# An encoder block of two SwiGLUs and a mixer on one core: two block products of four units ahead at the head of each SwiGLU, norms written in place on VectorE with four tiles in flight, and the shared accumulator of the down-projection added in pieces

## The chip, the cores and the metric

The kernel runs on one core of a Trainium2 chip. The metric is the device time of one execution in microseconds (us); a smaller one is better. A core has a matrix engine (TensorE, PE in the profile; its weight loads are PEld), VectorE (DVE), ScalarE (ACT), GpSimd (POOL) and SyncE (SP), which issues the transfers between HBM and the on-chip memory SBUF. Products of PE land in banks of a second on-chip memory, PSUM, and another engine reads ("evacuates") them from there. Each engine works through its own queue in order and waits on semaphores for the others.

## The reference

One layer over x of 1024 tokens by 1024 columns, fp32 in and out, with a hidden width of 2816:

```python
h = x
f1 = swiglu(rms_norm(h, ffn1_pre_g), ffn1_w_gate, ffn1_w_up, ffn1_w_down)
h = h + 0.5 * rms_norm(f1, ffn1_post_g)
mix = hybrid_mixer(rms_norm(h, mix_pre_g), ...)   # two kinds of attention, gated, projected
h = h + rms_norm(mix, mix_post_g)
f2 = swiglu(rms_norm(h, ffn2_pre_g), ffn2_w_gate, ffn2_w_up, ffn2_w_down)
h = h + 0.5 * rms_norm(f2, ffn2_post_g)

def rms_norm(x, g): return x * rsqrt(mean(x * x) + EPS) * g
def swiglu(x, w_gate, w_up, w_down): return (silu(x @ w_gate) * (x @ w_up)) @ w_down
```

## The kernel before, in words

The 1024 tokens are eight tiles of 128. Each fp32 matrix is split into a high and a low part of a shorter format (`xh` and `xl`, two halves of `wt`), and a product is three matmuls per pair of operands: high by high, high by low, low by high.

**Gate and up.** The 2816 columns of the gate and of the up matrix are 11 column pairs of 256; a pair of one of the two matrices is a unit (p, m), so a SwiGLU (FFN1, FFN2) has 22. A unit is computed with seven block products instead of eight (a Strassen-Winograd scheme over 2x2 blocks of x and of the weight). A product, numbered 0 to 6, is 12 matmuls of 128x512. Products 0 and 1 need only the upper half of x, that is token tiles 0 to 3, and weight blocks as loaded; the others need the lower half (block 2) or sums and differences of blocks (4, 5, 6, 3, made by `XS.put`, L414, and of the weight, L615 to L626). A weight block is cast to its high part by ACT (L648), and its low part is a subtraction on DVE (L649). Sums of the seven results are made on DVE (L697, L760 to L800), and the hidden values are written to HBM and read back for the down-projection. At the head of a SwiGLU the order is product 0 of units 0 and 1, product 1 of units 0 and 1, and then unit by unit.

**Making x.** A pre-norm takes a tile: ACT squares it with a sum (L441), POOL makes `rstd` from the sum (L307, L309), and the tile is scaled by `rstd` and the gain: DVE does the first columns (`on_dve`, L451) and ACT with POOL the rest (`on_pool`, L457, L458). PE transposes the scaled tile in blocks of 128x128 into a PSUM bank (L426), ACT copies out the high part (`xh`, L430), DVE subtracts for the low part (`xl`, L431), and the bank is free. There are four single banks (`B1`) and two double ones.

**Down.** Five groups of seven block products (order 0, 5, 1, 4, 6, 2, 3), each for four pairs of token tiles, are added into eight accumulators `acc` (1024 columns a tile) and a shared `bacc` of 512 columns, which belongs into three quarters of a tile pair's output. After the last group `fix` adds it: DVE to one half of tile tt (L1037), POOL to both halves of tile tt + 4 (L1039). What is left of the depth follows as 16 plain products of six matmuls (L283), one for each tile and column half, which DVE adds into `acc` (L1118).

**Turns.** When a tile of a SwiGLU or of the mixer is done, `postnorm` squares it (ACT, L499), multiplies it by its gain into a new tile `xn` (L488, some columns on POOL and the others on DVE), and adds it, scaled by `rstd`, to the residue `res` (DVE, L512, a scalar_tensor_tensor, STT). A pre-norm of the new residue for the next part follows. `norm_tok` lets two tiles be between these steps at a time.

**What sets the order.** The program is written as generators, one for each chain of steps. A planner, `Plan`, plays them through with costs for each engine's steps and ranks, and the order in which it starts them is the order of the program. Buffers are taken in that order from pools: 4 KB slots (`slot`), half slots, big slots for `xh` and `xl`. A changed cost, rank or number of tokens so moves instructions in every queue.

Of the kernel before, what the change touches and what calls it, by code (L numbers as in the profile page):

```python
# [10 lines left out]
F32R = mybir.dt.float32r  # L11
# [96 lines left out]
PRE1, PREM, PRE2 = 768, 768, D  # L108
POOL1, POOLM, POOL2 = [512] * 8, [384] * 8, [512] * 4 + [1024, 768, 512, 512]
# [3 lines left out]
HELD = 4  # L113

# [105 lines left out]
def _build(tc, es, a, consts, out, dbg):  # L220
# [133 lines left out]
    class XS:  # L354
# [25 lines left out]
        def put(self, t, xn, scaled, rank):  # L380
# [15 lines left out]
            else:  # L396
# [14 lines left out]
                tt = [slot([P, 2, 512], name="xt") for _ in range(2)]  # L411
                t1, t2, t3, t4 = tt[0][:, 0, :], tt[0][:, 1, :], tt[1][:, 0, :], tt[1][:, 1, :]
# [21 lines left out]
    def prenorm(src, g, X, t, rank, split_at, xn=None):  # L434
# [12 lines left out]
        m = split_at  # L447
        scaled = [Event(), Event((m > 512) + (m < D))]

        def on_dve(c0, c1, ev):  # L450
# [5 lines left out]
        def on_pool(c0, c1, ev):  # L456
            yield act(c1 - c0, lambda: A.mul(xn[:, c0:c1], src[:, c0:c1], rs[0]))  # L457
            yield pool(c1 - c0, lambda: G.tensor_mul(xn[:, c0:c1], xn[:, c0:c1], g()[:, c0:c1]))  # L458
            plan.set(ev)
# [11 lines left out]
    def postnorm(y, g, res_src, dst, t, box, junk, pool_cols, parts=1):  # L471
# [10 lines left out]

        m = pool_cols(t)
        gained = Event((m > 0) + (m < D))

        def gain_of(cols, eng):
            def write():
                eng.tensor_mul(xn[:, cols], y[:, cols], g()[:, cols])  # L488

            n = cols.stop - cols.start  # L490
            yield (pool if eng is G else dve)(n, write)
            plan.set(gained)

        xn = slot([P, D], name="xn")
        box.append(xn)
# [6 lines left out]
        if m:  # L502
            spawn(gain_of(slice(0, m), G), 0)
        if m < D:
            spawn(gain_of(slice(m, D), V), 8)
        yield act(D + 100, sq)
        yield from rstd_steps(bx[0], D, rs)
        yield gained
        n = D // parts
        for q in range(parts):  # L510
            cs = slice(n * q, n * q + n)
            yield dve(n, lambda: V.scalar_tensor_tensor(res[:, cs], xn[:, cs], rs[0], res[:, cs], op0=ALU.mult, op1=ALU.add))  # L512
            spawn(store(dst[t * P : (t + 1) * P, cs], res[:, cs], 512 // parts), 6)
# [30 lines left out]
    def ffn(X, wg, wu, wd, post, hs, hp, started=None, room=None):  # L544
        raw_tok, w_tok, hl_tok = Tokens(4 if room is None else 3), Tokens(6 if room is None else 2), Tokens(3)

        def more():
            yield room
            plan.release(raw_tok, 1)
            plan.release(w_tok, 4)  # L550
# [7 lines left out]
        seq = [(units[0], 0), (units[1], 0), (units[0], 1), (units[1], 1)]  # L558
        for n, u in enumerate(units):
            if n > 1:  # L560
# [3 lines left out]
            if n > 1:  # L564
# [5 lines left out]
        unit_tok = Tokens(2)  # L570
# [13 lines left out]
        def loads():  # L584
            yield 0.5
            for p, m in units:
# [11 lines left out]
        def prep():  # L598
            sums = {}

            def begin(u):
# [5 lines left out]
                bx.used = used = [Event(4), Event(4)]  # L607
# [29 lines left out]

            def one(u, i):
# [17 lines left out]
            for u, i in seq:  # L656
                if u not in sums:
                    begin(u)
                if i == 1:
# [55 lines left out]
        def step(u, i, ub):  # L715
# [21 lines left out]
            if i == 0:  # L737
# [16 lines left out]
            elif i == 5:  # L754
# [3 lines left out]
                def first():  # L758
                    yield ub.m1
                    yield dve(512, lambda: V.tensor_add(u2(), ub.b6, u2()))  # L760
# [128 lines left out]
        fixed = [Event() for _ in range(NT)]  # L889
# [133 lines left out]
        def evac(g, i, tt, ps, ev, tok):  # L1023
# [8 lines left out]
            if g == NGR - 1 and i == 3:  # L1032
                spawn(fix(tt), 2)
# [11 lines left out]
        pdone = [Event() for _ in range(4)]  # L1045

        def down():
            for g in range(NGR):
                evs = {}
                banks = {}  # L1050
                for s, i in enumerate(ORDER):
# [4 lines left out]
                    for tt in range(4):  # L1056
# [27 lines left out]
                        if g == NGR - 1 and i == 2:  # L1084
                            e = evs[i, tt] = pdone[tt]
# [85 lines left out]
    def begin():  # L1171
        def one(t):
# [9 lines left out]
            yield from prenorm(bx[0], lambda: gb["g1"], X1, t, 3, PRE1)  # L1182
# [12 lines left out]
    norm_tok = Tokens(2)  # L1195

    def post1(y, t):
# [8 lines left out]
        yield from postnorm(y, lambda: gb["p1"], a["x"], h1, t, bx, lambda: gb["j1"], POOL1.__getitem__)  # L1206
        yield from prenorm(bx[0], lambda: gb["gm"], Xm, t, 3, PREM, bx[1])
# [1193 lines left out]
    def merge():  # L2401
# [109 lines left out]
        def tail(y, t, ev):  # L2511
# [3 lines left out]
            yield from postnorm(y, lambda: gb["pm"], h1, h2, t, bx, lambda: gb["jm"], POOLM.__getitem__)  # L2515
            yield from prenorm(bx[0], lambda: gb["g2"], X2, t, 3, PRE2, bx[1])
# [97 lines left out]
```

## Time and profile before

| | |
|---|---|
| median of 3 runs | 2476.06 us (2475.08 to 2478.7) |
| the profiled execution | 2472.7 us, of which its span 2470.5 us |
| PE busy | 2310.1 us (94%) |
| DVE busy | 1602.3 us (65%) |
| ACT busy | 1042.7 us (42%) |
| POOL busy | 798.0 us (32%) |

The span is the time from the first to the last instruction in the trace; all positions in this document are microseconds from its start. FFN1's gate and up stand at 0 to 470, its down-projection at 470 to 707, the mixer (with attention) up to 1772, FFN2's gate and up from 1726 to 2206, its down-projection and the last norms to the end.

### The profile page before, as it was taken

The page shows a single profiled execution, that of the slowest core. Times are in us where ns is not written, and L with a number is a line of the kernel's source. Part 1 is how long each engine was busy: PE and PEld are TensorE (multiplying, and loading weights), DVE is VectorE, ACT ScalarE, POOL GpSimd, SP SyncE. Part 2 cuts the span into 40 slices and gives each one's busy share as a digit, 9 for nine tenths or more (in the row PEclk, how much of TensorE's full clock was granted, in tenths as well). Part 3 has the DMA queues.
Part 4 walks back from the last instruction along what each step waited for, and adds up shares of the span by engine and source line. Part 5 has one row for each costly group of instructions (what it writes and reads, how often), then busy time and mean ns, then how long its engine had stood idle before and what let it go on. Part 6 is the DMA issues. An engine that isn't in the chain of part 4 may idle for free. (4 is left out here: it accounts for less than half of the span.)

```text
span 2470.5 us, 30753 instructions
## 1 busy us (share of the span) xinstructions
PE 2310.1 (94%) x11096; PEld 1928.9 (78%) x11096; DVE 1602.3 (65%) x2667; ACT 1042.7 (42%) x1966; POOL 798.0 (32%) x600
## 2 busy tenths in 40 slices
PE   6999999999979999999998898988889999998996
PEld 4888888778869987888887777766678888877885
DVE  7887877756582105665666767258877877774657
ACT  6343434332153336666664555455343433433211
POOL 2000000354384445665623223566200000023535
PEclk8999999999989999999999999999989999999998
DMA  4243443677342132131232323665333534447762
GB/s 154 103 168 131 170 154 128 244 307 267 135 164 76 60 103 92 38 83 50 66 97 67 85 74 98 206 242 193 131 124 128 183 128 153 162 179 289 286 216 102
DMA packets 188823, 360.64 MB, mean 146 GB/s; under 512 B 32448, under 2 KB 104640, under 8 KB 188160
## 3 DMA queue, kind: packets, MB, share of 16 engines
q1 hardware_dynamic: 188672, 358.69, 42.5%
q8 instruction: 87, 1.43, 0.2%
q14 instruction: 64, 0.52, 0.1%
HBM read 237.92 MB, written 120.72 MB: 145 GB/s over the span
## 5 line engine op out<-in xcount | busy, mean ns | idle before, releaser
L675 PE MATMUL s<-xh,wt 128*128 128x512 f32 x1408 | 452.3, 392 | 13.2 <-DVE uu L771 12.2
L522 POOL TENSOR_TENSOR wdb<-rawd,wdb 128x1024 fp32r<-128x1024 f32 x34 | 87.0, 2562 | 957.9 <-ACT wdb L521 957.9
L675 PE MATMUL b<-xh,wt 128*128 128x512 f32 x1056 | 344.1, 393 | 1.8 <-DVE wt L649 0.8
L675 PEld LDWEIGHTS s<-xh,wt 128*128 128x128 f32 x1408 | 265.9, 189 | 71.9 <-issue 13.3
L675 PE MATMUL s<-xl,wt 128*128 128x512 f32 x704 | 275.4, 391 | 0.0
L675 PEld LDWEIGHTS b<-xh,wt 128*128 128x128 f32 x1056 | 199.8, 189 | 44.4 <-DVE wt L649 1.2
L675 PE MATMUL b<-xl,wt 128*128 128x512 f32 x528 | 207.0, 392 | 0.4 <-DVE xl L431 0.4
L1079 PE MATMUL b<-wdb,ha 128*128 128x512 f32 x864 | 203.2, 390 | 2.2 <-POOL wdb L522 2.2
L1079 PE MATMUL s<-wdb,ha 128*128 128x512 f32 x816 | 196.7, 396 | 8.6 <-POOL wdb L522 4.8
L1079 PEld LDWEIGHTS b<-wdb,ha 128*128 128x128 f32 x864 | 162.3, 188 | 36.8 <-POOL wdb L522 3.1
L1079 PEld LDWEIGHTS s<-wdb,ha 128*128 128x128 f32 x816 | 156.0, 192 | 43.9 <-POOL wdb L522 5.7
L1442 PE MATMUL b<-xh,wh 128*128 128x512 f32 x384 | 162.7, 424 | 1.4 <-DVE o L1963 0.8
L1913 POOL TENSOR_TENSOR p<-p,rd 128x1024 f32<-128x1024 f32 x64 | 122.4, 1921 | 118.0 <-DVE rd L1910 112.7
L649 DVE TENSOR_TENSOR wt<-s,wt 128x512 fp32r<-128x512 f32 x176 | 120.4, 712 | 53.7 <-ACT wt L648 53.7
L675 PEld LDWEIGHTS s<-xl,wt 128*128 128x128 f32 x704 | 133.2, 189 | 27.0
L1442 PE MATMUL b<-xl,wh 128*128 128x512 f32 x384 | 153.3, 399 | 0.0
L1442 PE MATMUL b<-xh,wl 128*128 128x512 f32 x384 | 153.2, 399 | 0.0
L522 POOL TENSOR_TENSOR wdb<-td,wdb 128x1024 fp32r<-128x1024 f32 x40 | 105.9, 2653 | 73.9 <-ACT wdb L521 73.9
L426 PE MATMUL b<-cst,p 128*128 128x128 f32 x768 | 107.2, 280 | 22.0 <-DVE ptd L431 14.8
L522 POOL TENSOR_TENSOR wl<-raw,wh 128x512 fp32r<-128x512 f32 (+3 forms) x88 | 109.7, 1263 | 53.8 <-ACT wh L521 46.3
L426 PEld LDWEIGHTS b<-cst,p 128*128 128x128 f32 x768 | 90.1, 143 | 39.8 <-DVE ptd L431 17.4
L648 ACT CAST wt<-s 128x512 fp32r<-128x512 f32 x176 | 103.2, 621 | 34.1 <-DVE s L619 16.8
(295 smaller groups left out, 5015.6 us busy)
## 6 DMA issues: line engine op xcount, KB each, us to landing
hs_d<-hl SPq DMA_DIRECT2D x140, 512.0 KB
ha<-hs_d SPq DMA_DIRECT2D x70, 1024.0 KB
raw<-in_ffn_w_gate_dram SPq DMA_DIRECT2D x44, 512.0 KB
raw<-in_ffn_w_up_dram SPq DMA_DIRECT2D x44, 512.0 KB
rawd<-in_ffn_w_down_dram SPq DMA_DIRECT2D x44, 512.0 KB
raw<-in_w_in_dram SPq DMA_DIRECT2D x28, 512.0 KB
h<-res SPq DMA_DIRECT2D x16, 512.0 KB
lg_d<-lg SPq DMA_DIRECT2D x32, 256.0 KB
```

The costliest lines, as they stand in the source:

```text
L426: T.transpose(b[:rows, i * P : (i + 1) * P], src(i), ident)
L522: yield pool(n, lambda: G.tensor_sub(lo, src, hi))
L648: yield act(512, lambda: A.copy(w[:, 0], src))
L649: yield dve(512, lambda: V.tensor_sub(w[:, 1], src, w[:, 0]))
L675: T.matmul(out(), l, r, start=(first and k == 0 and n == 0), stop=(k == 3 and n == 2), skip_group_check=True,)
L1079: T.matmul(ps, l, r, start=(fresh and n == 0), stop=(n == 5), skip_group_check=True)
L1442: T.matmul(bs.ps, l, r, start=(part == 0 and n == 0), stop=(part == 7 and n == 2))
L1913: yield pool(S, lambda: G.tensor_tensor(bx.p, bx.p, bx.rd.broadcast_to([P, S]), op=ALU.mult))
```

## The change

It has three parts.

1. *Four units ahead.* `EARLY = 4`: at the head of each SwiGLU products 0 and 1 of four units are done before all others, in the order 0.0, 1.0, 0.1, 1.1 and then 2.0, 3.0, 2.1, 3.1 (unit.product). Their weights come by four loads of their own (`ers`: 128x8x128, the 128 columns that products 0 and 1 need), cast and split in `head_of`; the later products load the whole unit as before. Four units may be open (`unit_tok`), product 0's result is copied to a half slot (`m1`), and the full slot `uu` is taken only at the first sum. In FFN2 four weight blocks may be open at the start, not two.
2. *Norms.* The post-norm multiplies the tile by its gain in place, 1024 columns on DVE, and the pre-norm writes its scaled tile there too, all columns on DVE (two steps of 512). POOL and ACT have no columns left. The differences of `XS.put` for blocks 4 and 3 are written over the old half of x. `NORM = 4` tiles may be in flight.
3. *The shared accumulator.* `fix` adds `bacc` on DVE, 512 columns at a time, as soon as a product's last sum is in: 24 steps, where there were 8 of DVE and 8 of POOL with 1024 columns.

```diff
-PRE1, PREM, PRE2 = 768, 768, D
-POOL1, POOLM, POOL2 = [512] * 8, [384] * 8, [512] * 4 + [1024, 768, 512, 512]
+EARLY = 4
+NORM = 4
+W0 = 4
...
-                tt = [slot([P, 2, 512], name="xt") for _ in range(2)]
-                t1, t2, t3, t4 = tt[0][:, 0, :], tt[0][:, 1, :], tt[1][:, 0, :], tt[1][:, 1, :]
+                tt = slot([P, 2, 512], name="xt")
+                t1, t2, t3, t4 = old[0], tt[:, 0, :], tt[:, 1, :], old[1]
...
-        spawn(on_dve(0, 512, scaled[0]), rank)
-        if m > 512:
-            spawn(on_dve(512, m, scaled[1]), rank)
-        if m < D:
-            spawn(on_pool(m, D, scaled[1]), rank)
+        for n in range(2):
+            spawn(scale(512 * n, 512 * n + 512, scaled[n]), rank)
...
-        if m:
-            spawn(gain_of(slice(0, m), G), 0)
-        if m < D:
-            spawn(gain_of(slice(m, D), V), 8)
+        def gain_of():
+            yield dve(D, lambda: V.tensor_mul(y, y, g()))
+            plan.set(gained)
+
         yield act(D + 100, sq)
+        spawn(gain_of(), 2)
...
-        seq = [(units[0], 0), (units[1], 0), (units[0], 1), (units[1], 1)]
+        early = units[:EARLY]
+        seq = [(early[n + j], i) for n in range(0, EARLY, 2) for i in range(2) for j in range(2)]
...
-        unit_tok = Tokens(2)
+        unit_tok = Tokens(EARLY)
+        ers = {u: (Box(), Event()) for u in early}
...
+            def head_of(u, i):
+                (ex, ee), wx = ers[u], ws[*u, i]
+                yield ee
+                w = wx[0].w = slot([P, 2, 4, P], F32R, "wt")
+                src = ex.r[:, 4 * i : 4 * i + 4, :]
+                yield act(512, lambda: A.copy(w[:, 0], src))
+                yield dve(512, lambda: V.tensor_sub(w[:, 1], src, w[:, 0]))
+                plan.set(wx[1])
+                if i == 1:
+                    plan.release(raw_tok)
...
-                        ub.uu = slot([P, 2, 512], name="uu")
-                        A.copy(ub.uu[:, 0, :], ub.b1)
+                        ub.c1 = half_slot([P, 512], name="m1")
+                        A.copy(ub.c1, ub.b1)
...
-        def fix(tt):
-            yield pdone[tt]
-            yield dve(512, lambda: V.tensor_add(Y[tt][:, 512:], Y[tt][:, 512:], bacc[tt]))
-            plan.set(fixed[tt])
-            yield pool(1024, lambda: G.tensor_add(
-                Y[tt + 4].rearrange("p (n c) -> p n c", n=2), Y[tt + 4].rearrange("p (n c) -> p n c", n=2),
-                bacc[tt][:, None, :].broadcast_to([P, 2, 512]),
-            ))
-            plan.set(fixed[tt + 4])
+        def fix(i, tt):
+            yield bdone[tt]
+            o = dst(KIND[i], tt)
+            yield dve(512, lambda: V.tensor_add(o, o, bacc[tt]))
+            plan.set(fixed[tt + (0 if i == 2 else 4)])
...
-    norm_tok = Tokens(2)
+    norm_tok = Tokens(NORM)
```

The first place is PE's queue around the last transposes of FFN1's head. A name like `xt` or `xn` behind `cst` is a block that is transposed, `wt` a split weight block, and `b` and `s` are PSUM banks. Before:

```order
L675 MATMUL b_425<-xh_144,wt_324 128x512
L426 MATMUL b_514<-cst,xt_303 128x128 x4
L426 MATMUL b_521<-cst,xt_338 128x128 x4
L426 MATMUL b_528<-cst,xt_317 128x128 x4
L675 MATMUL s_562<-xh_340,wt_456 128x512
L675 MATMUL s_654<-xh_340,wt_575 128x512
L426 MATMUL b_535<-cst,xt_338 128x128 x4
L675 MATMUL b_546<-xh_319,wt_406 128x512
```

After, `xn_105` and its like are the old halves, which now hold differences, and `b_525` is product 0 of unit 2:

```order
L685 MATMUL b_388<-xh_135,wt_197 128x512
L427 MATMUL b_476<-cst,xn_105 128x128 x4
L427 MATMUL b_485<-cst,xt_301 128x128 x4
L427 MATMUL b_491<-cst,xn_114 128x128 x4
L427 MATMUL b_498<-cst,xt_307 128x128 x4
L427 MATMUL b_509<-cst,xn_124 128x128 x4
L685 MATMUL s_620<-xh_329,wt_484 128x512
L427 MATMUL b_518<-cst,xn_149 128x128 x4
L685 MATMUL b_525<-xh_128,wt_283 128x512
```

In both the four products of units 0 and 1 are through when the last transposes come; the products of units 2 and 3 stand behind the last of them.

The second place is PE's queue ahead of the first transposes of the second half of FFN2's x: `wo` by `mt` are the last groups of the mixer's output projection. Before:

```order
L283 MATMUL b_15247<-wo_15033,mt_15015 128x512 x3
L283 MATMUL b_15247<-wo_15101,mt_15058 128x512 x3
L283 MATMUL b_15259<-wo_15033,mt_15015 128x512 x3
L283 MATMUL b_15259<-wo_15101,mt_15058 128x512 x3
L426 MATMUL b_15299<-cst,xn_15242 128x128 x4
L426 MATMUL b_15312<-cst,xn_15267 128x128 x4
```

After, where `b_15160` with `wt_15122` is product 1 of unit 3:

```order
L284 MATMUL b_15293<-wo_15029,mt_15012 128x512 x3
L284 MATMUL b_15293<-wo_15088,mt_15062 128x512 x3
L685 MATMUL b_15160<-xh_14629,wt_15122 128x512
L685 MATMUL b_15160<-xl_14630,wt_15122 128x512
L685 MATMUL b_15160<-xh_14629,wt_15122 128x512 x2
L685 MATMUL b_15160<-xl_14630,wt_15122 128x512
L685 MATMUL b_15160<-xh_14629,wt_15122 128x512 x2
L685 MATMUL b_15160<-xl_14630,wt_15122 128x512
L685 MATMUL b_15160<-xh_14629,wt_15122 128x512 x2
L685 MATMUL b_15160<-xl_14630,wt_15122 128x512
L685 MATMUL b_15160<-xh_14629,wt_15122 128x512
L427 MATMUL b_15365<-cst,y_14614 128x128 x4
```

A product of 12 matmuls has come between the last group of the output projection and the first transpose; the other three new products stand further ahead, among the groups of the output projection before the last eight.

The third place is DVE's queue at the end of FFN2, from the first tile's multiply by its gain on. Before (`acc` is a tile, `b` the bank of a plain product, `p` the gain):

```order
L488 TENSOR_TENSOR xn_20051<-acc_18763,p_3305_19985 128x512
L1118 TENSOR_TENSOR acc_18773<-acc_18773,b_19976 128x512
L512 SCALAR_TENSOR_TENSOR res_20022<-xn_20051,rstd_20069,res_20022 128x1024
L1118 TENSOR_TENSOR acc_18773<-acc_18773,b_19987 128x512
L488 TENSOR_TENSOR xn_20071<-acc_18773,p_3305_19985 128x512
L1118 TENSOR_TENSOR acc_18781<-acc_18781,b_19996 128x512
L512 SCALAR_TENSOR_TENSOR res_20032<-xn_20071,rstd_20115,res_20032 128x1024
```

After:

```order
L483 TENSOR_TENSOR acc_18755<-acc_18755,p_3333_19982 128x1024
L1129 TENSOR_TENSOR acc_18765<-acc_18765,b_19984 128x512
L493 SCALAR_TENSOR_TENSOR res_20018<-acc_18755,rstd_20062,res_20018 128x1024
L1129 TENSOR_TENSOR acc_18773<-acc_18773,b_19992 128x512
L1129 TENSOR_TENSOR acc_18773<-acc_18773,b_20000 128x512
L483 TENSOR_TENSOR acc_18765<-acc_18765,p_3333_19982 128x1024
L1129 TENSOR_TENSOR acc_18782<-acc_18782,b_20009 128x512
L483 TENSOR_TENSOR acc_18773<-acc_18773,p_3333_19982 128x1024
L1129 TENSOR_TENSOR acc_18782<-acc_18782,b_20020 128x512
L1129 TENSOR_TENSOR acc_18792<-acc_18792,b_20030 128x512
L493 SCALAR_TENSOR_TENSOR res_20028<-acc_18765,rstd_20078,res_20028 128x1024
```

The multiply has the whole width, and the second tile's STT (`res_20028`) has moved from six rows to ten rows behind the first multiply, with five evacuations and two multiplies between the two STTs.

## Rows read from the trace of the kernel before

**Rows 1.** The page, part 1: busy time, share and instructions of each engine.
```profile
PE 2310.1 (94%) x11096; PEld 1928.9 (78%) x11096; DVE 1602.3 (65%) x2667; ACT 1042.7 (42%) x1966; POOL 798.0 (32%) x600
```

**Rows 2.** Windows: each engine's busy time in a stretch, first head, steady, second head.
```profile
core 0: us, PE busy (x) PEld busy (x) DVE busy (x) ACT busy (x) POOL busy (x), PEclk, DMA share, GB/s
...
20.00:40.00 20.00, 11.73 (x43) 8.01 (x44) 19.02 (x30) 12.02 (x24) 8.31 (x12) 0.83 0.20 46
...
100.00:150.00 50.00, 50.00 (x221) 41.16 (x220) 48.78 (x100) 21.30 (x40) 0.00 (x0) 1.00 0.51 179
1761.00:1812.00 51.00, 34.32 (x147) 26.53 (x147) 45.03 (x66) 24.36 (x44) 12.72 (x20) 0.73 0.39 136
```

**Rows 3.** PE's waits, 0 to 60: us in total, times, longest.
```profile
PE b L426 <- DVE xl L431: 10.8, 10, 2.0
PE b L426 <- DVE xn L451: 7.8, 1, 7.8
```

**Rows 4.** PE's waits, 660 to 746, FFN1 to the mixer.
```profile
PE b L283 <- DVE xl L431: 9.1, 3, 5.1
PE b L283 <- DVE acc L1118: 5.8, 2, 3.1
```

**Rows 5.** PE's waits, 1690 to 1820, mixer to FFN2: the largest.
```profile
PE b L426 <- DVE xn L451: 9.9, 2, 6.2
```

**Rows 6.** PE's waits, 2400 to 2471, the end.
```profile
PE b L283 <- DVE acc L1118: 5.1, 4, 3.1
```

**Rows 7.** DVE's timeline at the turn to FFN1's down-projection: start, duration, instruction.
```profile
455.44 1.21 DVE L919 TENSOR_TENSOR td<-rawd,rawd 128x1024 f32<-128x1024 f32 x1
...
460.62 3.43 DVE L924 TENSOR_TENSOR td<-rawd,rawd 128x1024 f32<-128x1024 f32 x1
```

**Rows 8.** Line L488 on DVE in the SwiGLUs: duration in ns, min/median/max, and where.
```profile
L488 DVE TENSOR_TENSOR xn<-acc,p x15: 678/686/2308, 679.2 to 2464.2; 128x512 f32<-128x512 f32 x14, 128x256 f32<-128x256 f32 x1
```

**Rows 9.** DVE's timeline in the last stretch.
```profile
2427.12 0.69 DVE L1118 TENSOR_TENSOR acc<-acc,b 128x512 f32<-128x512 f32 x1 [0.67 <-PE b L283]
...
2462.98 1.28 DVE L512 SCALAR_TENSOR_TENSOR res<-xn,rstd,res 128x1024 f32<-128x1024 f32 x1
...
2465.58 1.42 DVE L512 SCALAR_TENSOR_TENSOR res<-xn,rstd,res 128x512 f32<-128x512 f32 x2 [0.72 <-POOL rstd L309]
```

**Rows 10.** DVE's timeline, FFN1 to the mixer; in brackets the idle time before.
```profile
685.32 2.27 DVE L512 SCALAR_TENSOR_TENSOR res<-xn,rstd,res 128x1024 f32<-128x1024 f32 x1 [3.83 <-POOL rstd L309]
...
719.35 2.88 DVE L512 SCALAR_TENSOR_TENSOR res<-xn,rstd,res 128x1024 f32<-128x1024 f32 x1
```

**Rows 11.** POOL's timeline, FFN1 to the mixer.
```profile
672.84 10.30 POOL L1039 TENSOR_TENSOR acc<-acc,bacc 128x1024 f32<-128x1024 f32 x4 [20.76 <-DVE acc L1028]
...
684.74 0.55 POOL L309 TENSOR_TENSOR rstd<-var,neg_half 128x1 f32<-128x1 f32 x1
```

**Rows 12.** PE's timeline, FFN1 to the mixer: plain products, then each pair's projections.
```profile
698.37 8.70 PE L283 MATMUL b<-wdb,hp 128*128 128x512 f32 x30 [2.79 <-DVE acc L1118]
...
713.26 0.58 PE L283 MATMUL b<-wh,xh 128*128 128x256 f32 x1 [1.83 <-DVE xl L431]
...
729.48 0.58 PE L283 MATMUL b<-wh,xh 128*128 128x256 f32 x1 [5.09 <-DVE xl L431]
...
740.79 0.39 PE L283 MATMUL b<-wh,xh 128*128 128x256 f32 x1 [2.14 <-DVE xl L431]
```

**Rows 13.** PE's timeline, mixer to FFN2: the last output groups, then transposes.
```profile
1761.52 11.04 PE L283 MATMUL b<-wo,mt 128*128 128x512 f32 x48
1776.23 0.63 PE L426 MATMUL b<-cst,xn 128*128 128x128 f32 x4 [3.67 <-DVE xn L451]
...
1795.01 1.09 PE L426 MATMUL b<-cst,xn 128*128 128x128 f32 x4 [6.23 <-DVE xn L451]
```

**Rows 14.** DVE's timeline: the last low half of FFN2's x.
```profile
1812.45 0.69 DVE L431 TENSOR_TENSOR xl<-b,xh 128x512 fp32r<-128x512 f32 x1
```

**Rows 15.** PE's timeline: the last transposes of FFN1's x.
```profile
60.14 0.60 PE L426 MATMUL b<-cst,xt 128*128 128x128 f32 x4
```

More of the change, by code (lines that the diff above doesn't have):

```diff
@@ L481, in postnorm @@
         res = box[0]
[L483 to L495, printed above, removed]
+        box.append(y)
+        gained = Event()
         def sq():
@@ L511, in postnorm @@
             cs = slice(n * q, n * q + n)
-            yield dve(n, lambda: V.scalar_tensor_tensor(res[:, cs], xn[:, cs], rs[0], res[:, cs], op0=ALU.mult, op1=ALU.add))
+            yield dve(n, lambda: V.scalar_tensor_tensor(res[:, cs], y[:, cs], rs[0], res[:, cs], op0=ALU.mult, op1=ALU.add))
             spawn(store(dst[t * P : (t + 1) * P, cs], res[:, cs], 512 // parts), 6)
@@ L585, in loads, with ld @@
             yield 0.5
+            for p, m in early:
+                yield raw_tok
+                ex, ee = ers[p, m]
+                def ld():
+                    ex.r = raw_tile((wg, wu)[m], 0, NK, 256 * p, P)
+                yield dma(512, ld)
+                plan.set(ee)
             for p, m in units:
@@ L606, in begin @@
                 bx.read2 = Event()
-                bx.used = used = [Event(4), Event(4)]
+                n = 3 if u in early else 4
+                bx.used = used = [Event(n), Event(n)]
                 def combos():
@@ L656, in prep @@
             for u, i in seq:
+                if u in early and i < 2:
+                    yield w_tok
+                    spawn(head_of(u, i), 7)
+                    continue
                 if u not in sums:
                     begin(u)
-                if i == 1:
+                if i == (5 if u in early else 1):
                     spawn(sums[u].combos(), 7)
@@ L759, in first, with add @@
                     yield ub.m1
-                    yield dve(512, lambda: V.tensor_add(u2(), ub.b6, u2()))
+                    def add():
+                        ub.uu = slot([P, 2, 512], name="uu")
+                        V.tensor_add(u2(), ub.b6, ub.c1)
+                    yield dve(512, add)
                     plan.release(B1)
@@ L888, in ffn @@
         bacc = [None] * 4
-        fixed = [Event() for _ in range(NT)]
+        fixed = [Event(1 if t < 4 else 2) for t in range(NT)]
         plain = [(Box(), Event(2)) for _ in range(2)]
@@ L1031, in evac @@
                 plan.release(tok)
-            if g == NGR - 1 and i == 3:
-                spawn(fix(tt), 2)
-        def fix(tt):
-            yield pdone[tt]
-            yield dve(512, lambda: V.tensor_add(Y[tt][:, 512:], Y[tt][:, 512:], bacc[tt]))
-            plan.set(fixed[tt])
-            yield pool(1024, lambda: G.tensor_add(
-                Y[tt + 4].rearrange("p (n c) -> p n c", n=2), Y[tt + 4].rearrange("p (n c) -> p n c", n=2),
-                bacc[tt][:, None, :].broadcast_to([P, 2, 512]),
-            ))
-            plan.set(fixed[tt + 4])
-        pdone = [Event() for _ in range(4)]
+            if g == NGR - 1 and i == 5:
+                plan.set(bdone[tt])
+            if g == NGR - 1 and i in (6, 2, 3):
+                spawn(fix(i, tt), 2)
+        bdone = [Event() for _ in range(4)]
+        def fix(i, tt):
[3 more added lines that the diff above has]
+            plan.set(fixed[tt + (0 if i == 2 else 4)])
         def down():
@@ L1181, in one @@
             yield gains0
-            yield from prenorm(bx[0], lambda: gb["g1"], X1, t, 3, PRE1)
+            yield from prenorm(bx[0], lambda: gb["g1"], X1, t, 3)
         spawn(one(0), 0)
@@ L2572, in post2 @@
         yield gains2
-        yield from postnorm(y, lambda: gb["p2"], h2, out, t, [], lambda: gb["j2"], POOL2.__getitem__, 2 if t == NT - 1 else 1)
+        yield from postnorm(y, lambda: gb["p2"], h2, out, t, [], lambda: gb["j2"], 2 if t == NT - 1 else 1)
     def second():
```

31 lines of the change are left out of this document (12 added, 19 removed).

## Prediction

> **What bounds the kernel now.** First the shares of the engines: TensorE (PE) is busy for 94% of the span, no other engine for more than 65% [rows 1]. So the matmuls set the end; the change leaves their number alone, and only PE's idle time can be won. Where that lies is read from what PE waits for, place by place. In the steady gate/up stretch there is none: PE 50.00 of 50.00 us [rows 2]. It lies at the turns: at the head of FFN1 (10.8 us for VectorE's low half of a split, `xl`, and 7.8 for its scaling L451) [rows 3], from FFN1 to the mixer (9.1 for `xl`, 5.8 for the evacuation L1118) [rows 4], from the mixer to FFN2 (9.9 for the scaling) [rows 5], and in the last stretch (5.1 for L1118) [rows 6], behind which the norms run out with PE done. The attention between keeps its order. The third view is VectorE at these turns: 19.02 of 20 us busy at the first head, 45.03 of 51 at the second [rows 2]. There it is itself the bound: what an edit gives it to do counts nearly in full, and what takes a wait out of its in-order queue gains nearly the whole wait.
>
> **The parts.** The sum is made against the profiled execution, 2472.7 us (2470.5 of span, 2.2 around it). That is 3.4 below the median of the runs, 2476.06, so 3.4 is added at the end.
>
> *What VectorE is given.* Of the post-norms, 24 multiplies of 1024 columns in place of 128x512 and 128x640 ones beside a part on GpSimd. No such multiply stands in before. The nearest row, an add of two SBUF inputs of 1024 columns, takes 1.21 us alone and 3.43 while GpSimd runs [rows 7]; the old one took 0.69 [rows 8]. That is (1.21 - 0.69) x 24 = 12.5 us. The pre-norm's scaling gets 256 columns more for 16 tiles: half of a 512-column step (0.6), 16 x 0.3 = 4.8. The shared accumulator takes 24 adds of 512 columns where it had 8: 16 x 0.6 = 9.6. **27 us in all**, lost in full if each falls on the path. In return GpSimd's 48 multiplies and 8 adds go, and with them a slowing of VectorE: the STT L512 (scalar_tensor_tensor, 1024 columns) takes 1.28 us with GpSimd idle [rows 9], 2.27 beside a GpSimd multiply [rows 10], 2.88 beside its splits. These rows have a rule beside them: the Trainium skill (SBUF — State Buffer, "Who interferes with whom") says that a VectorE instruction with two SBUF inputs contends with a GpSimd one that reads SBUF. By that rule moving GpSimd's part is worth about a microsecond for each of these STTs, and what the splits do is not cured; the rows say the same.
>
> *The last tail.* Before, four GpSimd adds stand in a row, 10.30 us, and the first tile's `rstd` behind them, at 684.74 in the first tail and as far behind in the last [rows 11]. VectorE waits 3.83 us for it at an STT ahead of the next evacuation [rows 10], and PE up to 3.1 for a bank [rows 6]. After, none of it is left, and VectorE's queue from the first evacuation on is 16 evacuations, one piece, eight multiplies and eight STTs: 17 x 0.6 + 8 x 1.2 + 8 x 1.2 = 29.4 us. From 2427.12 [rows 9], with 1.2 for what it still waits (a product of PE now and then, the square that must be done before y is overwritten), it ends at 2457.7. Before it was 2465.58 + 1.42 = 2467.0 [rows 9]. Of these 9.3 I take off 0.6 for stores of 512 KB that now leave closer together: **8.7**. The low bound is 4, if every multiply waits half a microsecond more for its square.
>
> *FFN1 to the mixer.* The plain products end at 698.37 + 8.70 = 707.1 [rows 12]. Without the 5.8 us of waits they end at 701, and at the pace of 1.38 us for six matmuls that PE has where it does not stall (11.04 for 48 [rows 13], against 8.70 for 30 here), at 697. VectorE's queue in that time (16 evacuations, two pieces, four multiplies, four STTs: 20.4 us alone) just fits into 16 x 1.38 = 22. Eight scalings more and the first pair of tiles reaches the projections at some 705, 8 us before 713.26 [rows 12]. Its matmuls, 8.4 us, end at 714; the second pair, which came at 729.48 after 5.09 of wait, is ready about then, since four tiles are in flight. The next pair (740.79 before) needs VectorE's four multiplies, four STTs and eight scalings of the last tiles: 14.4 us if alone, so 725 and a gain of 16; but GpSimd's splits of the projections' weights lie there (2.88 at 719.35 [rows 10]), and with half of the steps slowed it is 731. I take **10**, bounds 4 and 16.
>
> *Mixer to FFN2.* Four products more, 12 matmuls of 0.23 us each, 11 us in all, can run before the second half of x is there. In the new order three of them stand among the output projection's groups and push the last eight from 1761.52 to about 1769.8; the fourth stands ahead of the first transpose and fills most of the 3.67 us of wait there [rows 13]. From the start of the eight groups to the last `xl` it is 1812.45 - 1761.52 = 50.9 us [rows 13, 14], 6.23 of it a wait for the second pair of tiles, which two tokens hold back. With four tokens and no GpSimd step I count 4 us less (the 6.23 less the dearer multiplies). Net 11 - 8.3 + 4 = 6.7; I take **6**, bounds 1 and 10.
>
> *Head of FFN1.* The four new products stand behind the last transposes (PE's order above), so they fill none of the 18.6 us of waits; the last transpose, now at 60.14 [rows 15], must itself come earlier. VectorE sets it: the same 28 `xl` and 16 differences, 8 x 0.3 us more of scaling, three other steps fewer, and no scaling that waits for GpSimd. By a count of its queue up to the last `xl` I make its way **2.5** us shorter (0 to 5): 2.4 of scaling more, three steps (1.8) fewer, and some 3 us of waits for GpSimd and of slowed scaling saved. The four new loads take the places of the old ones around x's second half in SP's queue, so x is not later. Three differences now written over their operands cost nothing while the transposes that read them keep up.
>
> *Steady state.* The copy m1 now lies in one of seven half slots, and the full slot is taken at the first add. PE is full there and VectorE 48.78 of 50 [rows 2]: 0, if the order keeps PE fed.
>
> Sum: 8.7 + 10 + 6 + 2.5 = 27.2. 2472.7 - 27.2 = 2445.5, and 3.4: **2449 us** (-1.1%).
>
> **The rivals.** (a) *Given back at the inner turns.* The tail is won, but the splits slow VectorE's longer steps at both: 8.7 + 4 + 1 + 0 = 13.7, **2462**. For it: 2.88 and 3.43 stand in rows of such places. Against it: fewer GpSimd reads there. (b) *The extra products fill the gaps.* VectorE finishes x at FFN1's head early enough, and the second half at FFN2's waits less than I count: 5 us more at the one, 4 at the other, 4 from uncontended steps: **2436**. (c) *Slower: the multiplies are contended.* The 16 of the inner turns stand, 1024 columns wide, in the queue that PE waits for, at 3.43 instead of 1.21: 16 x 2.2 = 35 more, **2484**. It decides from 13 of 16 on (13 x 2.2 = 28, the whole sum). For it: the contended add of that shape [rows 7]; against it: GpSimd is idle for much of these turns. The Trainium skill speaks on its side (Perfetto Trace Analysis, "Optimizing Scalar/DVE Operations"): when VectorE is saturated, work may better be offloaded to ScalarE, and this change takes ScalarE's part of the scaling back; the same section says that offloading between VectorE and GpSimd might not help, and the STTs above fit that. (d) *No change.* The turns are won and steady state loses it: 22 units in each FFN, a stall of one 0.6 us step at each of the 44, 26 us: **2475**. VectorE's 48.78 of 50 speaks for it, the unchanged count of its steps there against.
>
> **How the numbers follow.** Forecast (2440 to 2456) 0.50; (a) 0.20; (b) 0.14; (c) 0.08; (d) 0.08. The range 2433 to 2466 holds the forecast, (a) and most of (b), and leaves out (c), (d) and the edges. About 0.2%, 5 us, is what a measurement of this kernel tells from no change: (d) is mostly "same", (c) slower, the others faster.
>
> **What would show it.** No 10.3 us of GpSimd adds at the tails, and no wait of 3.8 us ahead of the STT; multiplies near 1.2 us and STTs near 1.3; VectorE's last step some 9 us sooner after its first L1118 (now L1129) than the 40 us of before; PE's waits for L1118 gone; the first transpose of FFN2's second half without 3.67 of wait, and the second pair without 6.23. I am wrong if multiplies take 2.5 us or more at the inner turns, if PE waits for evacuations behind a multiply, or if gate/up shows waits that it did not have.

## The result, and the profile after

| | median | least to most | ratio to before, 95% interval |
|---|---|---|---|
| before, beside it | 2476.28 us | 2475.08 to 2478.70 (4) | |
| changed kernel | 2454.04 us | 2450.33 to 2458.65 (4) | 0.9913 [0.9899, 0.9927] |

The change makes the kernel 22.2 us faster (0.87%); 2449 was forecast. The profiled execution is the slowest of the four, 2458.65 us, 4.6 above the median, where that of before was 3.6 below the median beside it. So the two spans, 2456.8 and 2470.5, are only 13.7 us apart, and the places below add up to that; the other 8.5 us of the 22.2 cannot be placed.

The page of the changed kernel, part 1, beside [rows 1]:

```profile
PE 2306.5 (94%) x11096; PEld 1927.9 (78%) x11096; DVE 1598.0 (65%) x2684; ACT 1039.7 (42%) x1950; POOL 740.5 (30%) x552
```

GpSimd loses 48 instructions and 57.5 us, and VectorE has no more busy time than before, although it took GpSimd's work over. The lines by form show why (count, then total us and mean ns, then the idle time before them):

```profile
L493 DVE SCALAR_TENSOR_TENSOR res<-acc,rstd,res 128x1024 f32<-128x1024 f32 x15 | 18.9, 1278 | 1.0 <-POOL rstd L310 0.7
...
L483 DVE TENSOR_TENSOR y<-y,pm 128x1024 f32<-128x1024 f32 x8 | 9.7, 1219 | 0.6 <-ACT junk L479 0.6
```

The STT, 2.27 and 2.88 in [rows 10], takes 1.28 everywhere, and the multiply 1.22 (one of the 24, at the turn from FFN1 to the mixer, 3.43). For 3.83 us ahead of one STT [rows 10] there are now 0.7 us of waits for `rstd` ahead of all of them.

**The end.** DVE's timeline, beside [rows 9]:

```profile
2421.77 0.69 DVE L1129 TENSOR_TENSOR acc<-acc,b 128x512 f32<-128x512 f32 x1
...
2427.03 1.29 DVE L493 SCALAR_TENSOR_TENSOR res<-acc,rstd,res 128x1024 f32<-128x1024 f32 x1
...
2448.63 3.80 DVE L493 SCALAR_TENSOR_TENSOR res<-acc,rstd,res 128x1024 f32<-128x1024 f32 x4
```

From the first evacuation to the last step it is 2452.43 - 2421.77 = 30.7 us; before 39.9. PE has no wait left from 2380 on; its 96 matmuls of the plain products stand in one row:

```profile
2420.21 21.92 PE L284 MATMUL b<-wdb,hp 128*128 128x512 f32 x96
```

The span ends 4.4 us behind VectorE, before 3.5.

**The turns.** PE's waits in the windows 0 to 60, 640 to 760 and 1660 to 1840, beside [rows 3 to 5] (us in total, times, longest):

```profile
PE b L427 <- DVE xn L451: 9.4, 2, 8.0
PE b L427 <- DVE xl L432: 9.2, 6, 2.9
...
PE b L427 <- DVE xl L432: 7.6, 3, 5.0
PE b L427 <- DVE acc L451: 6.7, 4, 2.0
...
PE b L427 <- DVE y L451: 8.5, 2, 5.1
PE b L427 <- ACT y L2516: 3.9, 2, 3.5
```

At the turn from FFN1 to the mixer the waits for evacuations are gone, but PE now waits 14.3 us ahead of transposes (L427), for a bank that `xl` has to free or for a scaled tile. PE's timeline there:

```profile
702.04 2.64 PE L427 MATMUL b<-cst,acc 128*128 128x128 f32 x16 [1.44 <-DVE acc L451]
705.96 0.66 PE L427 MATMUL b<-cst,acc 128*128 128x128 f32 x4 [1.27 <-DVE xl L432]
707.88 2.57 PE L427 MATMUL b<-cst,acc 128*128 128x128 f32 x12 [1.26 <-DVE xl L432]
710.10 0.56 PE L284 MATMUL b<-wh,xh 128*128 128x256 f32 x1
...
729.55 1.94 PE L427 MATMUL b<-cst,acc 128*128 128x128 f32 x8 [1.84 <-DVE acc L451]
736.52 3.67 PE L427 MATMUL b<-cst,acc 128*128 128x128 f32 x16 [5.04 <-DVE xl L432]
739.85 0.56 PE L284 MATMUL b<-wh,xh 128*128 128x256 f32 x1
```

A tile is eight transposes. Thirty-two of them, four tiles, stand ahead of the first projection at 710.10. The 96 projections of these two pairs follow without a wait up to 722.6; before, the same 96 ended at 736.9. Then the next four tiles come as one batch too. VectorE makes all of their scalings (L451) before the first `xl` of these tiles, which frees a bank:

```profile
734.45 1.41 DVE L451 SCALAR_TENSOR_TENSOR acc<-res,rstd,gm 128x512 f32<-128x512 f32 x2 [0.45 <-POOL rstd L310]
735.78 3.20 DVE L432 TENSOR_TENSOR xl<-b,xh 128x512 fp32r<-128x512 f32 x5
```

So their first projection starts at 739.85, where before had it at 740.79 [rows 12].

**A place outside the sum.** The start of the second of the five groups of each down-projection. PE's waits from 480 to 560, then 2180 to 2400 without its first row:

```profile
PE s L1092 <- POOL wdb L503: 5.8, 2, 4.0
PE s L1092 <- ACT wdb L502: 3.6, 2, 1.9
...
PE s L1092 <- POOL wdb L503: 5.8, 2, 4.0
PE s L1092 <- ACT wdb L502: 3.6, 2, 2.0
```

In the first window before had 2.5 and 0.5 for GpSimd's split, 1.1 for `bacc` and 0.3 for ScalarE's. DVE's timeline shows what the splits come behind; a `td` is a difference of weight blocks from which the weight of a later product of the group is split, and the second `td` is made from the first. First the changed kernel:

```profile
520.62 1.28 DVE L1043 TENSOR_TENSOR bacc<-bacc,s 128x512 f32<-128x512 f32 x2 [18.54 <-PE s L1092]
521.82 1.22 DVE L934 TENSOR_TENSOR td<-rawd,rawd 128x1024 f32<-128x1024 f32 x1
523.22 1.28 DVE L1043 TENSOR_TENSOR bacc<-bacc,s 128x512 f32<-128x512 f32 x2 [0.18 <-PE s L1092]
524.42 3.21 DVE L937 TENSOR_TENSOR td<-rawd,td 128x1024 f32<-128x1024 f32 x1
```

Then before:

```profile
514.93 1.23 DVE L919 TENSOR_TENSOR td<-rawd,rawd 128x1024 f32<-128x1024 f32 x1 [10.13 <-DMA rawd<-in_ffn_w_down_dram]
523.51 1.29 DVE L1028 TENSOR_TENSOR bacc<-bacc,s 128x512 f32<-128x512 f32 x2 [7.36 <-PE s L1079]
524.71 1.74 DVE L922 TENSOR_TENSOR td<-rawd,td 128x1024 f32<-128x1024 f32 x1
```

Before, the first `td` is made at 514.93, as soon as its block has landed, and VectorE is idle again before the sums. Now the first sum of products stands ahead of it in the in-order queue: VectorE idles 18.54 us for PE, and the splits of ScalarE and GpSimd are behind it. GpSimd's timeline:

```profile
524.20 2.36 POOL L503 TENSOR_TENSOR wdb<-td,wdb 128x1024 fp32r<-128x1024 f32 x1 [5.63 <-ACT wdb L502]
526.51 3.33 POOL L503 TENSOR_TENSOR wdb<-rawd,wdb 128x1024 fp32r<-128x1024 f32 x1
```

PE's wait of 4.0 us ends at 529.90, just after the second of these, which splits a block as loaded. It stands in GpSimd's queue behind the split of the first `td`, which VectorE could have made 9 us earlier (e5 below makes it at 512.39).

**The places added up.** PE's matmuls of the two profiles were paired in their order; the difference of their starts gives where PE gains (+) and loses (-):

| place | us |
|---|---|
| head of FFN1 | +4.2 |
| FFN1, gate/up to down | -1.4 |
| FFN1, down (start of the 2nd group) | -5.9 |
| FFN1 to the mixer | +5.0 |
| attention | -2.1 |
| mixer to FFN2 | +9.6 |
| FFN2, to the end of down's 2nd group | -4.0 |
| last stretch, PE | +7.9 |
| the rest | +0.5 |

PE ends 13.2 us earlier; the row "the rest" is what follows it. The attention's drift is in this execution alone; the profiles of the variants of the changed kernel below don't have it. FFN1's down row can be read from two rows of 24 matmuls on either side of that place, in PE's timeline, first of before and then of the changed kernel:

```profile
482.08 5.60 PE L1079 MATMUL s<-wdb,ha 128*128 128x512 f32 x24
539.52 5.60 PE L1079 MATMUL b<-wdb,ha 128*128 128x512 f32 x24
```

```profile
479.38 5.60 PE L1092 MATMUL s<-wdb,ha 128*128 128x512 f32 x24
542.68 5.60 PE L1092 MATMUL b<-wdb,ha 128*128 128x512 f32 x24
```

They stand 57.44 us apart before and 63.30 after. In FFN2 the same rows are 58.15 apart (2231.41 to 2289.56) and 62.74 (2221.47 to 2284.21), a loss of 4.6, of which the table's row to the group's end keeps 4.0.

### The profile page after: what moved, and what is told of

Same layout as the page of the kernel before. It is cut to its first block, busy times and chain, and to the rows that moved or that the text cites. A ratio compares the mean times of both kernels' runs of the same rounds, so it can differ in the third digit from the quotient of the medians.

```text
span 2456.8 us, 30660 instructions
## 1 busy us (share of the span) xinstructions
PE 2306.5 (94%) x11096; PEld 1927.9 (78%) x11096; DVE 1598.0 (65%) x2684; ACT 1039.7 (42%) x1950; POOL 740.5 (30%) x552
## 5 line engine op out<-in xcount | busy, mean ns | idle before, releaser
L685 PE MATMUL s<-xh,wt 128*128 128x512 f32 x1408 | 453.6, 392 | 14.3 <-DVE uu L786 13.8
L427 PE MATMUL b<-cst,p 128*128 128x128 f32 x768 | 108.4, 282 | 20.1 <-DVE ptd L432 13.4
L427 PEld LDWEIGHTS b<-cst,p 128*128 128x128 f32 x768 | 90.8, 144 | 38.4 <-DVE ptd L432 16.6
```

What stands on the lines that cost most here:

```text
L427: T.transpose(b[:rows, i * P : (i + 1) * P], src(i), ident)
L685: T.matmul(out(), l, r, start=(first and k == 0 and n == 0), stop=(k == 3 and n == 2), skip_group_check=True,)
```

## The experiments

The theory at first was the prediction's: the tails are won by taking the GpSimd adds out, four tiles in flight help at the turns, and little is lost elsewhere. The rival: the four tiles hurt, and a queue order costs 5 us in each down-projection. Ratios are to before, which ran on the same chip each time. The variants are of the changed kernel except where before is named.

**e1, two units ahead in place of four.**

```diff
-EARLY = 4
+EARLY = 2
-W0 = 4
+W0 = 2
```

> The changed kernel with EARLY = 2 and W0 = 2: products 0 and 1 of two units ahead, all else as changed. My theory: at FFN2's head the two extra pairs of products are worth what they fill there, 11 us of matmuls less the 8.3 by which three of them push the output projection, and some of the wait that is left: 4 to 7 us; at FFN1's head nothing, since they stand behind the last transposes. So 2458 to 2461. Rival 1: the whole gain of both heads (14 us in the profile) is theirs: 2468. Rival 2: the norms and the four tiles in flight made it all: 2454, no change.

2458.62 us (2457.22 to 2465.57), 0.9939 [0.9919, 0.9958]: 4.6 above the changed kernel, with overlapping intervals. PE's gain is 2.9 in place of 4.2 at the head of FFN1 and the same 9.5 at FFN2's, so beside four tiles in flight the new products are worth little there.

**e2, two tiles in flight; e7, three.** `NORM = 2` and `NORM = 3` in place of 4, nothing else.

> The changed kernel with two tiles in flight instead of four. My theory: at FFN2's head the second pair of tiles waits again (6.2 us before), at the turn to the mixer the second pair too (5.1): 8 to 10 us slower than the change, 2462 to 2464. Rival: VectorE is the limit at both turns, so tiles in flight only change the order: within 3 us of 2454.

> The changed kernel with three tiles in flight. My theory: with more tiles in flight VectorE and ScalarE take each step for all of them before the next step, so the first tile's transposes come later and PE's projections come in batches; three lies between: 2444 to 2451. Rival: the two tokens are an accident of one order, and three is no better than four: 2452 to 2456.

e2: 2441.13 us (2439.66 to 2442.14), 0.9862 [0.9847, 0.9877], 12.9 below the changed kernel. The theory falls. e7: 2449.73 (2449.30 to 2451.66), 0.9898 [0.9881, 0.9915], in between. Windows of 700 to 740, of before, of the changed kernel and of e2 (the columns are those of [rows 2]):

```profile
700.00:740.00 40.00, 29.15 (x171) 26.04 (x169) 34.98 (x36) 22.63 (x44) 34.73 (x36) 0.80 0.57 187
```

```profile
700.00:740.00 40.00, 25.73 (x164) 22.76 (x163) 35.98 (x40) 24.63 (x44) 29.55 (x26) 0.78 0.62 214
```

```profile
700.00:740.00 40.00, 32.39 (x223) 30.24 (x222) 32.81 (x34) 25.07 (x47) 27.98 (x28) 0.96 0.56 182
```

PE does 223 matmuls in place of 164, and 0.96 of the clock is granted in place of 0.78; these are means of its two levels, 1.00 (2.4 GHz) and 0.50 (1.2 GHz). In e2's timeline of PE eight transposes, one tile, are followed at once by projections:

```profile
700.27 1.03 PE L427 MATMUL b<-cst,acc 128*128 128x128 f32 x8
701.54 0.38 PE L284 MATMUL b<-wh,xh 128*128 128x256 f32 x1 [0.24 <-ACT xh L431]
```

VectorE begins the first tile's scaling at 689.65; with four in flight it begins six scalings together at 701.24. The turn gains 17.1 us on before in place of 5.0, by the pairing of the table above; with three tiles (e7) it gains 12.3.

**e10, four tiles in flight in the kernel before.** `norm_tok = Tokens(4)` in place of 2.

> The kernel before with four tiles in flight, one number changed. My theory: the steps of four tiles come in batches there too, and PE's projections and transposes with them: 8 to 13 us slower than before, 2484 to 2489. Rival: with ScalarE and GpSimd taking part of the norms, VectorE has room and more tiles in flight help, as the 6.2 us wait for the second pair suggests: 2465 to 2472.

2488.97 us (2488.76 to 2490.49), 1.0050 [1.0035, 1.0065]: 12.1 slower, in the range expected, and with nothing else of the change in it. But the loss is not where it was expected. Paired with before, its PE loses 0.9 us at the turn from FFN1 to the mixer, 7.5 inside the mixer (850 to 915 in before) and 5.0 at the turn to FFN2. In the mixer PE waits for `qr`, a step of GpSimd that starts at 887.82 before and at 896.02 now, behind weight splits and steps on `pj`; and 0.83 of the clock is granted from 900 to 920, where it was 1.00. PE's waits from 880 to 930:

```profile
PE b L1750 <- POOL qr L1284: 3.3, 2, 2.1
```

So in the kernel before four tiles cost as much as in the changed one, but little of it at the turn to the mixer; the largest part comes of an order that they moved elsewhere.

**e8, two tiles and two units ahead** (both edits of e1 and e2).

> The changed kernel with two tiles in flight and only two units ahead (EARLY = 2, W0 = 2). My theory: where x comes tile by tile the extra products have less of a gap to fill, and the two runs with four tiles differ by 4.6 us only: 2441 to 2446. Rival: at FFN2's head PE waits longer for scaling with two tiles in flight (10.6 us), so the extra products are worth more there: 2447 to 2452.

2443.58 us (2441.54 to 2446.71), 0.9872 [0.9856, 0.9888]: 2.4 above e2, and the spreads overlap. By the medians the products of units 2 and 3 bring 2 to 5 us in all, little more than the spread. In the profiles, with two tiles in flight, they do fill a gap at the turn to FFN2: from 1640 to 2000 PE gains 12.6 us in e2 and 7.5 in e8.

**e3, the shared accumulator as before.** `fix(tt)` with one add of VectorE and one of GpSimd with 1024 columns, as the diff's removed lines have it.

> The changed kernel with the shared accumulator added as before: one step of 512 columns on VectorE and one of 1024 on GpSimd for each tile pair, after the last product. My theory: GpSimd's four adds, 10.3 us in a row, stand ahead of the first rstd again at both tails: 7 to 9 us at the last one, 3 to 6 at the turn to the mixer, so 2464 to 2469, with VectorE waiting for rstd at its first STT. Rival: the gain of the tail came from the norms that no longer wait for GpSimd's multiplies: under 3 us, 2457 at most.

2456.57 us (2455.68 to 2459.29), 0.9927 [0.9912, 0.9941]: 2.5 above the changed kernel, not 10 to 15. GpSimd's and then DVE's timeline at the last tail:

```profile
2412.92 9.83 POOL L1058 TENSOR_TENSOR acc<-acc,bacc 128x1024 f32<-128x1024 f32 x4 [20.76 <-DVE acc L1043]
...
2423.97 0.55 POOL L310 TENSOR_TENSOR rstd<-var,neg_half 128x1 f32<-128x1 f32 x1
```

```profile
2420.48 3.36 DVE L483 TENSOR_TENSOR acc<-acc,p 128x1024 f32<-128x1024 f32 x1
...
2424.55 1.28 DVE L493 SCALAR_TENSOR_TENSOR res<-acc,rstd,res 128x1024 f32<-128x1024 f32 x1
```

The four adds of 9.83 us and `rstd` behind them are back, but VectorE's STT starts at 2424.55, right behind `rstd`, with no wait in front of it, and PE has none in the whole stretch: by the pairing it gains 7.7 us there, and the changed kernel 7.9. The multiply beside GpSimd does take 3.36, so VectorE loses 2.1 us there all the same, but by then it has done one evacuation more than before.

**e4, half of the post-norm's multiply on GpSimd.** 512 columns on each engine, in place:

```diff
...
-            yield dve(D, lambda: V.tensor_mul(y, y, g()))
+            yield (pool if eng is G else dve)(512, lambda: eng.tensor_mul(y[:, cs], y[:, cs], g()[:, cs]))
...
-        spawn(gain_of(), 2)
+        spawn(gain_of(G, slice(0, 512)), 0)
+        spawn(gain_of(V, slice(512, D)), 2)
...
```

> The changed kernel with the post-norm's multiply in place split again: 512 columns on GpSimd (1.28 us) and 512 on VectorE. My theory: VectorE's reads of SBUF are slowed beside GpSimd's, so its 0.6 us saved per tile is lost in slower STTs (2.3 in place of 1.28) and multiplies (1.66 in place of 0.69), and rstd queues behind GpSimd's multiplies: 2457 to 2464. Rival: VectorE is the bound at the turns and any step taken off it helps: 24 x 0.6 us less, of which two thirds on the path, 2444 to 2449.

2463.38 us (2458.83 to 2468.86, 6 runs), 0.9956 [0.9938, 0.9973]: 9.3 above the changed kernel. The traces do not divide these 9.3, since the two profiled executions are only 1.5 us apart in their spans (2458.3 and 2456.8): that of e4 lies 3.3 below its median. The last stretch gains the same 7.9. The largest loss in this trace, 6.0 us, stands in the mixer at the place of e10's, again with PE waiting for `qr` (3.4 us). One of e4's lines by form:

```profile
L494 DVE SCALAR_TENSOR_TENSOR res<-acc,rstd,res 128x1024 f32<-128x1024 f32 x15 | 23.2, 1550 | 5.6 <-POOL rstd L310 5.2
```

The STT takes 1.55 us in the mean, and 5.2 of waiting for `rstd`, which follows GpSimd's multiply, is back. This agrees with the rule of the Trainium skill (SBUF — State Buffer, "Who interferes with whom") that was weighed before: without GpSimd's reads the step costs 1.28. How much of the 9.3 it makes is not shown.

**e9, both e3 and e4.**

> The changed kernel with both of GpSimd's parts at the tails back: the shared accumulator added as before, and 512 columns of each multiply in place. My theory: the last stretch gained 8 us because GpSimd has no longer both in its queue; with one of them alone (the two runs before) the gain stayed, with both PE waits for L1118's successor again, 4 to 8 us, and the time is 2467 to 2472. Rival: the order did it (the multiply now comes after the square and at a higher rank, so the first STT no longer stands ahead of the evacuations): no wait in the last stretch, 2461 to 2466.

2466.84 us (2464.36 to 2469.73), 0.9959 [0.9944, 0.9974], between the two ranges. Over the last stretch PE waits 1.6 us, not the 5.1 of [rows 6], and still gains 5.7 of the 7.9, although both of GpSimd's parts are back. So most of the tail is not theirs, and the theory falls here too. Nor is it the number of tiles: e2 with two gains 7.9 there, and e10, before with four, nothing. What still differs from before is that each multiply is queued behind its square, and with it one more evacuation ahead of the first STT; that this carries the tail is argued from the order, and no run has it alone. Nor does a run put back the wider parts (1024 and 768 columns) that GpSimd had of two later tiles.

**e5, `td` ahead of the sums.** In the second group of the down-projection the sums of its first product into `bacc` are held behind the first two `td` in VectorE's queue:

```diff
...
+                if g == 1 and i == 0:
+                    yield tds[1]
+                    yield dve(512, lambda: tc.keep_in_program_order(V.tensor_add(o, o, ps)))
...
```

> The changed kernel with VectorE's first three weight differences of the second down group (td) queued ahead of that group's first sums into bacc, as before the change the first of them was. My theory: the 9.4 us that PE waits there in each SwiGLU, 5 to 6 more than before, come from td standing behind sums that wait for PE: 5 to 7 us back in each, 2441 to 2444. Rival: the weights come late from HBM, and the order only shows it: 2454.

2438.67 us (2435.18 to 2441.63), 0.9850 [0.9834, 0.9867]: 15.4 below the changed kernel and below the range expected, with one place in the order of two SwiGLUs moved. DVE's timeline there:

```profile
512.39 1.23 DVE L935 TENSOR_TENSOR td<-rawd,rawd 128x1024 f32<-128x1024 f32 x1 [10.71 <-DMA rawd<-in_ffn_w_down_dram]
...
520.19 1.28 DVE L1047 TENSOR_TENSOR bacc<-bacc,s 128x512 f32<-128x512 f32 x2
```

PE's rows that stood 63.30 us apart start at 478.98 and 534.80, 55.82 apart: 7.5 us are won there, 1.6 more than the change had lost, for in before the second `td` stood behind the first sums too.

**e11, the half slot `m1` alone, in before.** Product 0's result goes into a half slot, and `uu` is taken at the first sum.

> The kernel before with only this of the change: product 0's result is copied to a half slot, and the unit's full slot is taken at its first sum. In the queue of VectorE this alone puts td of the second down group behind the first bacc sums. My theory: it costs what the order costs there, 5 to 6 us in each SwiGLU: 2485 to 2488. Rival: a slot taken later lets loads start earlier and gives that back: 2473 to 2479.

2483.30 us (2478.82 to 2485.61, 10 runs), 1.0026 [1.0016, 1.0035]: 6.4 slower. PE's waits from 480 to 560:

```profile
PE s L1084 <- POOL wdb L522: 5.8, 2, 4.0
PE s L1084 <- ACT wdb L521: 3.7, 2, 2.0
```

They are those of the changed kernel almost to the tenth, and DVE's queue has the same order as there. So it is this buffer edit that moved `td` behind the sums. In the profiles PE loses 5.4 and 4.3 us at the two places, and the span is 10.7 longer (2481.2 and 2470.5). The medians are only 6.4 apart, because the profiled execution of before lies 4.2 below the median beside e11.

**e6, e2 and e5, and the last `uu` ahead of another `td`** (the change from gate/up to down, where PE waits 6.7 us for `uu` behind a `td` of 3.35; 6.1 in before).

> The changed kernel with two tiles in flight, td of the second down group ahead of the bacc sums, and the last unit's second sum (uu) ahead of the last weight difference of the first down group, which waits for GpSimd. My theory: 13 us from the tiles as measured, 10 to 14 from td, and most of the 6.7 us that PE waits for uu in each SwiGLU, 8 to 12: 2416 to 2424. Rival: what PE gains at these places it loses again because the down group's weights are then late (GpSimd's splits of 2.4 to 3.4 us set them): 2432 to 2441.

2425.62 us (2421.72 to 2428.72), 0.9797 [0.9780, 0.9815], the fastest of all, though 1.6 us above the range expected. e2 and e5 by themselves add up to 2454.0 - 12.9 - 15.4 = 2425.7, so the third edit adds nothing that shows in the median. `uu` is 6.7 us earlier, but PE then waits for a weight that is late from HBM (ScalarE's timeline in FFN1, then PE's):

```profile
507.30 1.04 ACT L502 CAST wdb<-rawd 128x1024 fp32r<-128x1024 f32 x1 [2.68 <-DMA rawd<-in_ffn_w_down_dram]
```

```profile
508.40 0.73 PE L1105 MATMUL s<-wdb,ha 128*128 128x512 f32 x2 [4.40 <-ACT wdb L502]
```

**e12, e6 with the shared accumulator as before.**

> The fastest kernel so far (two tiles in flight, td and uu in front) with the shared accumulator added as before the change. My theory: the pieces are worth 0 to 3 us, since VectorE no longer stands at an STT for the first rstd: 2424 to 2429 against 2425.6. Rival: with less waiting elsewhere GpSimd's 10 us of adds reach the end again: 2430 to 2434.

2428.95 us (2422.84 to 2429.79), 0.9799 [0.9780, 0.9818]: 3.3 above e6, and the spreads overlap. In the last stretch PE gains 7.7, as in e3, and 7.9 in e6. With e3's 2.5 the pieces are worth some 3 us, or nothing.

## Why the prediction was right, and where it was not

It held in sign and size: 22.2 us measured of the 27.2 summed. The terms did not hold equally, and part of the agreement is luck: one term was 5.0 too large, two were 5.3 too small together, and some 10 us of loss stood in no term. Two of the signs that were named did not come: at the turn to FFN2 the first transpose still waits 3.41 us, of 3.67, and the second pair 5.09, of 6.23.

*The last tail, 8.7.* PE gains 7.9, VectorE's way is 9.2 shorter, and 0.9 goes to the stores (0.6 was taken off). The size is right, the mechanism was not: the four GpSimd adds were named as what holds `rstd` and so the bank, and e3 puts them back for 2.5 us, with 7.7 of the stretch still won. The step that failed is the one from "VectorE waits 3.83 us for it at an STT ahead of the next evacuation" to "After, none of it is left": the adds can stay, and the wait is gone. Its cause is argued only: it hangs on how early the STT stands in VectorE's queue. With the changed order a `rstd` that comes 8.9 us after PE's first plain product (e3), where it was 9.8 before, makes nobody wait.

*FFN1 to the mixer, 10.* 5.0 in the profile, near the low bound of 4. The first half came nearly as put: the first projection starts at 710.10, where 705 was put and 713.26 was before, and the second pair is ready with it. The step that failed is "and with half of the steps slowed it is 731", from 14.4 us of VectorE's steps for the next pair. VectorE takes from 712.19 to 735.86 for these multiplies, STTs and scalings, 23.7 us, with one of them slowed to 3.43 and with waits for `rstd` between them. Only then come the `xl` that free the banks, so the next pair's first projection starts at 739.85, 0.9 us before the old one. Four tokens let the planner put a step of four tiles one behind the other on each engine: six scalings at 701.24, 32 transposes from 702, and the same again. e2 gains 12.9 by undoing this, with 17.1 at this turn in its profile. e10 loses 12.1 by four tiles alone, but at other places.

*Mixer to FFN2, 6.* 9.6. The last eight groups start at 1764.54 and not at 1769.8, and the last `xl` ends at 1813.3, 0.2 later than before, with four products more done by then. So PE had more idle time ahead of the eight groups than I counted (12.0 us of waits from 1640 to 1726 before, 7.2 after). That the fourth product "fills most of the 3.67 us" failed: 3.41 is still there [rows 13]. So did the 4 us counted for four tokens at the wait of 6.23; 5.09 of it is left (PE's timeline):

```profile
1781.71 0.63 PE L427 MATMUL b<-cst,y 128*128 128x128 f32 x4 [3.41 <-DVE y L451]
...
1788.76 1.09 PE L427 MATMUL b<-cst,y 128*128 128x128 f32 x4 [5.09 <-DVE y L451]
```

By e1 the turn gains as much with two units ahead: its last eight groups end at 1765.0 and its last `xl` at 1802.0, so by what is left it is the norms' part of the change that helps, and of it not the four tiles: with two, e2 gains 12.6 there. No run has this part alone.

*Head of FFN1, 2.5.* 4.2, of which e1 gives 1.3 to the new products; the last transposes start at 54.90, for 60.14 [rows 15].

*Steady state, 0.* Right for gate/up, where PE has no new waits. The step that failed is "0, if the order keeps PE fed": the order does not, 50 us later. The half slot moved `td` (e11), and PE loses 5.9 and 4.6 us in the down-projections by the pairs of rows. Putting it right is worth 15.4 in the time (e5), of which some 3 us are more than was lost. The order had been read at the turns and not there.

*The rivals.* (c) is dead: of the 24 multiplies one takes 3.43, the others 1.2. (a) has it right that much is given back at the turn to the mixer, by batching and only in part by splits beside longer steps; at the turn to FFN2, where it has 1, 9.6 are won. (d) has a loss away from the turns, of less than half its size (26) and in another stage. (b), 2436, has its time nearly reached by e2, though not by its mechanism: without the extra products e8 is only 2.4 above e2.

## What to carry to other kernels

More tiles in flight are no gain by themselves: where a scheduler fills queues by step, they come through as one batch, and the engine that should be fed gets nothing and then everything; try two, three and four. A buffer taken later, or of another size, is an edit of every queue: after such a change read what stands ahead of each long wait on the in-order engines also in stages that the diff does not touch (`td` here, `qr` in e10 and e4). Test the parts of a change singly: this one was worth 22 us as it stood and 50 with two of its parts put right.

## What the runs showed of the hardware

- From 730 to 740 the changed kernel's PE has a granted clock of 0.50, the lower of its two levels (1.2 GHz), after it was busy for 4.76 of the 10 us before. From 750 to 760, where it works without a gap, it has 1.00 (2.4 GHz). A 256-column matmul takes 0.41 us at 710.89, where 0.50 is granted, and 0.28 from 711.99 on, where 1.00 is.
- A VectorE difference of 1024 columns from SBUF takes 1.22 us at 521.82 and 3.21 at 524.42 in the same kernel, with GpSimd's splits running beside the second. So does e3's multiply: 3.36 at 2420.48, most of it beside GpSimd's adds, and 1.22 in the median of the changed kernel.
- Executions of the changed kernel spread over 8.3 us (2450.33 to 2458.65); e2's over 2.5.
